# Every other quad of weight pieces of the gate and up products in Strassen's seven-product form

## The chip, the cores and the metric

The kernel runs on one core of one Trainium2 chip. The metric is the device time of one execution in microseconds (us). Three runs of the kernel before took 2240.97, 2241.1 and 2241.2 us, with 2241.1 us as the median. A core has TensorE (PE in the profile; PEld is its loading of stationary operands), VectorE (DVE), ScalarE (ACT), GpSimd (POOL) and SyncE (SP), which here issues the loads. Each engine works through its own instructions in a fixed order and waits where an operand or a buffer is not ready.

## The reference

One decoder layer over 256 tokens of width 2048 in float32. Two feed-forward blocks ("ffn1" and "ffn2", inner width 5632) stand before and after a mixing part (sliding-window attention beside a gated recurrence); a gated embedding and a last norm follow. Only the two feed-forward blocks are changed:

```python
def rmsnorm(x, w):
    return x * rsqrt(mean(x * x, axis=-1) + EPS) * w

def swiglu(h, w_gate, w_up, w_down):
    return (silu(h @ w_gate) * (h @ w_up)) @ w_down

x = x + 0.5 * swiglu(rmsnorm(x, ffn_norm), w_gate, w_up, w_down)
```

## The kernel before, in words

Every weight matrix comes from memory in pieces of 128 partitions x 1024 float32 values (512 KB): two blocks of 128 rows by 512 columns. Each value is used as a sum of two parts in a rounded float32 format. `Weights.prep` makes them for piece i: a DMA into `raw` (six buffers), a copy by ScalarE into `whi` (line 83, five buffers), and a subtraction on VectorE, `wlo` = `raw` - `whi` (line 84, five buffers). The activations are split the same way into a high and a low part (`hT*`, `act`).

The product of one piece with the activations takes twelve matmuls of 128 x 512 (`mm_a`): for each of the piece's two row blocks and each half `t` of the tokens, high by high (L241), low by high (L242), high by low (L247). The sums of a block of 512 output columns stand in two PSUM banks `pa`, one for each token half, out of four with the tag "acc"; four more with the tag "misc" serve transposes and small products.

The feed-forward block takes the inner width in 11 groups `c` of 512 columns. A group has eight gate and eight up pieces. ScalarE applies SiLU to the gate sums (L303), VectorE multiplies with the up sums (L310), and two later steps transpose the result on TensorE (L284) and split it into `act` (L285, L286). After six groups, and after the other five, the down products of those groups follow, and VectorE adds their sums to `x` (L317). The norm's scale 1/rms is applied after the gate and up products, so that they can begin on the unscaled input; for ffn1 that input also comes already transposed from memory (`xT`).

The weights stand in one list, `weight_order`, in which they are used. `Weights.next` hands out the next piece and first calls `prep` for up to four pieces ahead (AHEAD); the instructions of a prep get a high priority. Work such as the transposes is put off by a number of pieces with `W.later`. A scheduler then lists the instructions of each engine once, at build time, by these priorities and by its own estimate of when each could start; on the chip the order is fixed. The change touches `Weights.prep`, `FF_SLICES`, `weight_order`, `ffn`, `next_stage` and what comes before the two blocks.

## Time and profile before

| what | value |
|---|---|
| median of three runs | 2241.1 us |
| the profiled execution's own time | 2238.86 us |
| its span, first to last instruction | 2236.9 us |
| mean granted TensorE clock | 0.999 of full speed |
| PE busy | 2220.7 us (99%) |
| DVE busy | 1204.4 us (54%) |
| ACT busy | 1028.7 us (46%) |
| memory traffic | 187 GB/s on average |

One execution is profiled. "Busy" counts the time in which at least one instruction of the engine was under way; a matmul's record (some 390 ns) is longer than the distance between two of them, since they overlap in the array, so that the distance of their starts is what one costs. The idle time before an instruction, and who ended it, stands behind "|" in tables and in brackets in timelines. An order of instructions is given in other rows, without times.

### The profile page before, as it was taken

The numbers are of one execution on the slowest core, as the hardware profiler recorded it, in microseconds if no ns is written. First come the engines' busy times: TensorE is split into PE (matmuls) and PEld (weight loads), VectorE is DVE, ScalarE is ACT, GpSimd is POOL, SyncE is SP. The second block draws the span as 40 slices with busy tenths as digits, with TensorE's granted clock in tenths as the row PEclk, the third lists the DMA queues.
The fourth block names the chain that finished last, engine by engine and source line by source line (L and its number), as shares of the span: only waits on it lengthen the run. The fifth ranks groups of instructions, "written<-read, shape, count | busy, mean of one in ns | idle before, by whom it ended". The sixth has DMA issues, their size and how long they took to land.

```text
span 2236.9 us, 27361 instructions
## 1 busy us (share of the span) xinstructions
PE 2220.7 (99%) x10620; PEld 1837.4 (82%) x10620; DVE 1204.4 (54%) x1416; ACT 1028.7 (46%) x1294; POOL 12.0 (1%) x25
## 2 busy tenths in 40 slices
PE   9999999999999999999999999999999999999998
PEld 7888888888888888877888888888888888888887
DVE  6555544454455576776455555544554444445555
ACT  6544433444444445556444445444443344444454
POOL 0000000000000000000000000000000000000000
PEclk9999999999999999999999999999999999999999
DMA  8666666666665555545666655566666666666663
GB/s 314 203 195 192 189 191 193 195 191 188 188 188 187 182 169 151 160 133 160 193 189 190 193 186 186 187 190 192 190 187 191 196 190 188 190 192 204 187 191 109
DMA packets 118066, 418.92 MB, mean 187 GB/s; under 512 B 13745, under 2 KB 14129, under 8 KB 117937
## 3 DMA queue, kind: packets, MB, share of 16 engines
q1 hardware_dynamic: 117072, 415.83, 60.6%
q8 instruction: 83, 1.36, 0.3%
q10 hardware_dynamic: 864, 1.35, 0.2%
q14 instruction: 47, 0.38, 0.0%
HBM read 415.03 MB, written 2.10 MB: 186 GB/s over the span
## 4 chain that ended last, share of the span: by engine, by line
PE 99%; ACT 0%; issue 0%; DMA 0%; DVE 0%; SPq 0%; ACTq 0%; POOLq 0%; POOL 0%
PE pa L241 31%; PE pa L242 30%; PE pa L247 30%; PE pb L262 3%; PE pb L264 1%; PE tp L284 1%; PE lv L631 1%; PE tx L332 0%; PE sc L549 0%; DMA raw<-in_ffn_gate 0%; PE po L588 0%; PE pb L266 0%; PE pt L574 0%; ACT s L564 0%; ACT whi L83 0%
## 5 line engine op out<-in xcount | busy, mean ns | idle before, releaser
L84 DVE TENSOR_TENSOR wlo<-raw,whi 128x1024 fp32r<-128x1024 f32 (+1 forms) x781 | 955.2, 1223 | 928.5 <-ACT whi L83 924.4
L83 ACT CAST whi<-raw 128x1024 fp32r<-128x1024 f32 (+1 forms) x781 | 821.9, 1053 | 1114.2 <-PE pa L242 1039.1
L241 PE MATMUL pa<-whi,hTf 128*128 128x512 f32 x1408 | 552.8, 393 | 5.5 <-ACT whi L83 5.5
L242 PE MATMUL pa<-whi,hTf 128*128 128x512 f32 x1408 | 549.0, 390 | 0.0
L247 PE MATMUL pa<-wlo,hTf 128*128 128x512 f32 x1408 | 376.8, 389 | 0.0
L241 PEld LDWEIGHTS pa<-whi,hTf 128*128 128x128 f32 x1408 | 264.9, 188 | 60.2 <-ACT whi L83 6.2
L247 PEld LDWEIGHTS pa<-wlo,hTf 128*128 128x128 f32 x1408 | 264.4, 188 | 55.1
L242 PEld LDWEIGHTS pa<-whi,hTf 128*128 128x128 f32 x1408 | 265.0, 188 | 53.9
L241 PE MATMUL pa<-whi,act 128*128 128x512 f32 x704 | 275.9, 392 | 0.0
L242 PE MATMUL pa<-whi,act 128*128 128x512 f32 x704 | 274.1, 389 | 0.0
L241 PE MATMUL pa<-whi,hTmx 128*128 128x512 f32 x480 | 192.1, 400 | 0.0
L247 PE MATMUL pa<-wlo,act 128*128 128x512 f32 x704 | 188.3, 389 | 0.0
L242 PE MATMUL pa<-whi,hTmx 128*128 128x512 f32 x480 | 187.4, 391 | 0.0
L247 PEld LDWEIGHTS pa<-wlo,act 128*128 128x128 f32 x704 | 132.2, 188 | 27.5
L242 PEld LDWEIGHTS pa<-whi,act 128*128 128x128 f32 x704 | 132.2, 188 | 26.9
L241 PEld LDWEIGHTS pa<-whi,act 128*128 128x128 f32 x704 | 132.2, 188 | 26.9
L247 PE MATMUL pa<-wlo,hTmx 128*128 128x512 f32 x480 | 128.4, 389 | 0.0
L241 PEld LDWEIGHTS pa<-whi,hTmx 128*128 128x128 f32 x480 | 90.1, 188 | 21.4 <-issue 2.5
L247 PEld LDWEIGHTS pa<-wlo,hTmx 128*128 128x128 f32 x480 | 90.1, 188 | 18.9
L242 PEld LDWEIGHTS pa<-whi,hTmx 128*128 128x128 f32 x480 | 90.2, 188 | 17.4
L262 PE MATMUL pb<-hTmx,whi 128*128 128x512 f32 x240 | 67.6, 400 | 0.0
L241 PE MATMUL pa<-whi,hTpl 128*128 128x512 f32 (+1 forms) x160 | 53.9, 348 | 0.0
(207 smaller groups left out, 1471.7 us busy)
## 6 DMA issues: line engine op xcount, KB each, us to landing
raw<-in_ffn_up SPq DMA_DIRECT2D x176, 512.0 KB, 3.6
raw<-in_ffn_down SPq DMA_DIRECT2D x176, 512.0 KB, 3.6
raw<-in_ffn_gate SPq DMA_DIRECT2D x175, 512.0 KB, 3.6
raw<-in_w_ga SPq DMA_DIRECT2D x32, 512.0 KB, 3.5
raw<-in_w_gb SPq DMA_DIRECT2D x32, 512.0 KB, 3.5
raw<-in_w_out SPq DMA_DIRECT2D x32, 512.0 KB, 3.5
raw<-in_ple_gate SPq DMA_DIRECT2D x32, 512.0 KB, 3.7
raw<-in_w_i SPq DMA_DIRECT2D x16, 512.0 KB, 3.6
```

Of the source, the lines that this page charges most:

```text
L83: nc.scalar.copy(hi[:, c], raw[:, c])
L84: nc.vector.tensor_tensor(lo[:, c], raw[:, c], hi[:, c].bitcast(F32), op=ALU.subtract)
L241: nc.tensor.matmul(ps[t], ks[:, 0, tok], hi[:, c], start=(j == 0 and c == 0), stop=False)
L242: nc.tensor.matmul(ps[t], ks[:, 1, tok], hi[:, c], start=False, stop=False)
L247: nc.tensor.matmul(ps[t], ks[:, 0, tok], lo[:, c], start=False, stop=(last and c == 1))
L262: nc.tensor.matmul(ps, hi[:, c], mov(c), start=(first and c == 0), stop=False)
L264: nc.tensor.matmul(ps[:, 0:S], lo[:, c], mov(c)[:, 0], start=False, stop=False)
L284: nc.tensor.transpose(pt[:, c, t * P:(t + 1) * P], srcs[t][:, i * P:(i + 1) * P], ident)
L631: nc.tensor.matmul(ps[a * 64:a * 64 + 64, i], k[:, c], q[:, c], start=True, stop=True)
```

## The change

In 21 of the 22 groups (all but the first of ffn1) the gate and up products are made together. A "quad" is two gate pieces and two up pieces of the same four row blocks; a group has four. The quads alternate (PATTERN = "SPSP"): "P" quads are multiplied as before. "S" quads are read as a 2 x 2 matrix of blocks (row halves by gate and up), which is multiplied with the 2 x 2 matrix of activations (token halves by row halves) in the seven-product form of Strassen and Winograd. The seven weight operands are three of the four pieces and four sums of pieces (L101, VectorE, in place in `raw`); `prep` makes a high and a low part of each of the seven ("role" 0 to 6). One role takes six matmuls. The sums stand in eight banks over both kinds of quad: P1, P2, Q3, Q6 in "acc", Q7, Q5, P4 and PE_ in "misc"; P2, P4, Q3 and PE_ also take the P quads' sums. One ScalarE copy and eight VectorE operations (L402) make gate and up results out of them.

Since a product of this form mixes token halves, the activations have to be scaled by 1/rms before: `scaled_parts` scales `x`, transposes it on TensorE (L342), and for S quads forms four differences and splits them (L369, L373, L374). For ffn1 this is put off to pieces 9 to 12 of the first group, which still multiplies `hT` from `xT`, and the loads of `x` are moved forward; for ffn2 the scale comes from the first three quarters of `x`, and a factor for the rest is applied after the products. Loads are taken out of `prep` (`load`) and run three pieces ahead (LEAD) with eight `raw` buffers. The down products come in five slices per block, each of groups finished earlier. `hT` now lies in the pool of `act` tiles (23 instead of 17).

```diff
-ACTS = 17
+LEAD = 3
+ACTS = 23
...
+        if key[0] == "S":
+            _, first, second, q, role = key
+            if role > 3:
+                return
+            (name, nb), kg = ((first, 2 * q), (first, 2 * q + 1), (second, 2 * q + 1), (second, 2 * q))[role]
+            idx = (kg, nb)
...
+            raw = self.raws[i] = self.tile("raw", i, 8, F32)
+            n = 1024 // parts
+            for p in range(parts):
+                c = slice(p * n, (p + 1) * n)
+                self.nc.sync.dma_start(raw[:, c], src[:, c])
...
+        while self.loaded < min(i + 1 + (LEAD if i > 12 else 0), len(self.order)):
+            self.load(parts)
...
+            role = key[-1] if key[0] == "S" else 0
+            raws = [self.raws.get(i - role + k) for k in range(4)]
+            src = raws[(0, 1, 2, 0, 2, 3, 1)[role]]
+            if role == 3:
+                b11, b21, b22, b12 = raws
+                add(b22, b12, b22)
+                add(b12, b11, b12)
+                add(b11, b11, b22)
+            elif role == 6:
+                add(raws[1], raws[1], raws[0])
+            hi, lo = self.tile("whi", i, 5), self.tile("wlo", i, 5)
...
+                nc.scalar.copy(hi[:, c], src[:, c])
+                nc.vector.tensor_tensor(lo[:, c], src[:, c], hi[:, c].bitcast(F32), op=ALU.subtract)
...
-FF_SLICES = [(0, 6), (6, 11)]
+FF_SLICES = (((0, 3), (0, 2)), ((3, 5), (2, 4)), ((5, 7), (4, 6)), ((7, 9), (6, 8)), ((9, 11), (8, 11)))
+PATTERN = "SPSP"
...
+                for q, kind in enumerate(PATTERN):
+                    if kind == "S":
+                        order.extend(("S", (g, c), (u, c), q, role) for role in range(7))
+                    else:
+                        order.extend((v, (2 * q + k, c)) for k in range(2) for v in (g, u))
...
+        xs = [etile(name="xs") for _ in range(2)]
+        for t in range(2):
+            nc.scalar.activation(xs[t], x[t][q], AF.Copy, scale=s[:, t:t + 1])
...
+        full = [atile([P, 4, 2, P], F32, name="af") for _ in range(2)]
...
+                nc.scalar.activation(quarter[:, kp, c], pt[:, c].rearrange("p (t n) -> p t n", t=2), AF.Copy, scale=gain[:, f:f + 1])
+        a11, a21, a12, a22 = (quarter[:, k, :, t] for k in range(2) for t in range(2))
+        a5, a6, a7, a3 = (full[1][:, i] for i in range(4))
+        for o, u, v in ((a5, a21, a22), (a6, a11, a5), (a7, a21, a11), (a3, a12, a6)):
+            nc.vector.tensor_tensor(o, u, v, op=ALU.subtract)
+        parts = []
+        for i in range(2):
+            hi, lo = (atile([P, 4, 2, P], name="as") for _ in range(2))
+            nc.scalar.copy(hi, full[i])
+            nc.vector.tensor_tensor(lo, full[i], hi.bitcast(F32), op=ALU.subtract)
+            parts.append((hi, lo))
...
+        mix = lambda i: lambda c: (ch[:, i, c], cl[:, i, c])
+        A[q] = (raw(0, 0), raw(1, 0), mix(3), mix(1), mix(2), mix(0), raw(1, 1))
...
+        P1, P2, Q3, Q6, Q7, Q5, P4, PE_ = range(8)
...
+                for role in range(7):
+                    hi, lo = (v.rearrange("p (c n) -> p c n", c=2) for v in W.next(("S", first, second, q, role)))
+                    for c in range(2):
+                        sh, sl = A[q][role](c)
+                        mm(role, sh, hi[:, c])
+                        mm(role, sl, hi[:, c])
+                    for c in range(2):
+                        mm(role, A[q][role](c)[0], lo[:, c])
+                if q == PATTERN.rindex("S"):
+                    tmp = atile([P, 2, 512], F32, name="st")
+                    p1, v2 = tmp[:, 0], tmp[:, 1]
+                    nc.scalar.copy(p1, banks[P1])
+                    tt(v2, banks[Q6], p1, ALU.subtract)
+                    tt(g[:, 1], banks[Q7], v2, ALU.add)
+                    tt(u[:, 0], banks[Q5], v2, ALU.add)
+                    tt(u[:, 1], banks[Q5], g[:, 1], ALU.add)
...
+                    for (name, nb), (b0, b1) in ((first, (P2, P4)), (second, (Q3, PE_))):
+                        hi, lo = (v.rearrange("p (c n) -> p c n", c=2) for v in W.next((name, (2 * q + k, nb))))
+                        for c in range(2):
+                            for t, b in enumerate((b0, b1)):
+                                tok = slice(t * P, (t + 1) * P)
+                                mm(b, A[q][k][:, c, 0, tok], hi[:, c])
+                                mm(b, A[q][k][:, c, 1, tok], hi[:, c])
+                        for c in range(2):
+                            for t, b in enumerate((b0, b1)):
+                                mm(b, A[q][k][:, c, 0, t * P:(t + 1) * P], lo[:, c])
+        tt(g[:, 0], banks[P2], p1, ALU.add)
+        last_first(g, 0)
+        tt(g[:, 1], banks[P4], g[:, 1], ALU.subtract)
+        last_first(g, 1)
+        tt(u[:, 0], banks[Q3], u[:, 0], ALU.add)
+        tt(u[:, 1], banks[PE_], u[:, 1], ALU.add)
+        return g, u
...
+                e, u = strassen_group((gate, c), (up, c), A, silu)
                 for t in range(2):
-                    nc.vector.scalar_tensor_tensor(e[t], pu[t], r[:, t:t + 1], e[t], op0=ALU.mult, op1=ALU.mult)
+                    if n == 1:
+                        nc.vector.tensor_tensor(e[:, t], u[:, t], e[:, t], op=ALU.mult)
...
-            W.later(5 + 2 * nb + t, lambda t=t, nb=nb: load_x(t, nb))
+            W.later(4 + nb, lambda t=t, nb=nb: load_x(t, nb))
...
+    for q in range(4):
+        W.later(9 + q, lambda q=q: scaled_parts(A1, q, r_first(), gains["ffn1"]))
...
+        if nb == 2:
...
+            nc.vector.tensor_reduce(v3, ss2[:, :, 0:3], axis=AX.X, op=ALU.add)
+            nc.vector.tensor_scalar(v3, v3, 1.0 / 1536, EPS, op0=ALU.mult, op1=ALU.add)
+            nc.gpsimd.tensor_tensor(s3, v3, nhalf[:, 0:2], op=ALU.pow)
+            nc.vector.tensor_tensor(v3, v3, s3, op=ALU.mult)
...
+            for q in range(3):
+                W.later(1 + 2 * q, lambda q=q: scaled_parts(A2, q, s3, gains["ffn2"]))
...
+            W.later(2, lambda: scaled_parts(A2, 3, scale2[0], gains["ffn2"]))
```

The scheduler's order of TensorE, within the second group of a slice. Before, the twelve matmuls of one gate piece (`whi_801`, `wlo_802`) go to two banks:

```order
L241 MATMUL pa_822<-whi_801,hTf_82 128x512
L242 MATMUL pa_822<-whi_801,hTf_82 128x512
L241 MATMUL pa_823<-whi_801,hTf_82 128x512
L242 MATMUL pa_823<-whi_801,hTf_82 128x512
L241 MATMUL pa_822<-whi_801,hTf_82 128x512
L242 MATMUL pa_822<-whi_801,hTf_82 128x512
L241 MATMUL pa_823<-whi_801,hTf_82 128x512
L242 MATMUL pa_823<-whi_801,hTf_82 128x512
L247 MATMUL pa_822<-wlo_802,hTf_82 128x512
L247 MATMUL pa_823<-wlo_802,hTf_82 128x512
L247 MATMUL pa_822<-wlo_802,hTf_82 128x512
L247 MATMUL pa_823<-wlo_802,hTf_82 128x512
```

Now two roles of an S quad (`as` are the activations' parts, `ps_2041` and `ps_2042` are P1 and P2):

```order
L399 MATMUL ps_2041<-whi_2137,as_493 128x512
L399 MATMUL ps_2041<-whi_2137,as_494 128x512
L399 MATMUL ps_2041<-whi_2137,as_493 128x512
L399 MATMUL ps_2041<-whi_2137,as_494 128x512
L399 MATMUL ps_2041<-wlo_2138,as_493 128x512 x2
L399 MATMUL ps_2042<-whi_2153,as_493 128x512
L399 MATMUL ps_2042<-whi_2153,as_494 128x512
L399 MATMUL ps_2042<-whi_2153,as_493 128x512
L399 MATMUL ps_2042<-whi_2153,as_494 128x512
L399 MATMUL ps_2042<-wlo_2154,as_493 128x512 x2
```

A prepared operand of an S quad lasts for six matmuls to one bank, one of before for twelve to two banks.

VectorE's order around the end of a group and the start of the next. Before (`ff_982` and `ff_983` take the products of the gate and up results, `act` is their split):

```order
L84 TENSOR_TENSOR wlo_1116<-raw_1114,whi_1115 128x1024 [waits DMAHW6_49,PE_49,Activation_49]
L310 SCALAR_TENSOR_TENSOR ff_982<-pa_986,rstdf_498,ff_982 128x512 [waits PE_49]
L84 TENSOR_TENSOR wlo_1140<-raw_1138,whi_1139 128x1024 [waits DMAHW7_49,PE_49,Activation_49]
L310 SCALAR_TENSOR_TENSOR ff_983<-pa_987,rstdf_498,ff_983 128x512
L84 TENSOR_TENSOR wlo_1158<-raw_1156,whi_1157 128x1024 [waits DMAHW0_49,PE_49,Activation_49]
L84 TENSOR_TENSOR wlo_1176<-raw_1174,whi_1175 128x1024 [waits DMAHW1_49,PE_49,Activation_49]
L286 TENSOR_TENSOR act_820<-tp_866,act_820 128x2x256 [waits Activation_49]
```

Now (`wlo_1999` belongs to role 2 of the next group's first S quad, `wlo_2018` to role 3, `wlo_2053`, `wlo_2065` and `wlo_2078` to roles 4 to 6; `ps_1710`, `ps_1715`, `ps_1711` are P2, P4 and Q3 of the ending group):

```order
L118 TENSOR_TENSOR wlo_1999<-raw_1946,whi_1998 128x1024 [waits DMAHW4_49,PE_49,Activation_49]
L101 TENSOR_TENSOR raw_1946<-raw_1964,raw_1946 128x1024 [waits DMAHW5_49,DVE_49]
L402 TENSOR_TENSOR ff_1716<-ps_1710,st_1958 128x512 [waits PE_49]
L101 TENSOR_TENSOR raw_1964<-raw_1922,raw_1964 128x1024 [waits DVE_49]
L402 TENSOR_TENSOR ff_1716<-ps_1715,ff_1716 128x512 [waits PE_49]
L101 TENSOR_TENSOR raw_1922<-raw_1922,raw_1946 128x1024 [waits DVE_49]
L402 TENSOR_TENSOR ff_1717<-ps_1711,ff_1717 128x512 [waits PE_49]
L101 TENSOR_TENSOR raw_1934<-raw_1934,raw_1922 128x1024 [waits DVE_49]
L118 TENSOR_TENSOR wlo_2018<-raw_1922,whi_2017 128x1024 [waits Activation_49]
L118 TENSOR_TENSOR wlo_2053<-raw_1946,whi_2052 128x1024 [waits PE_49,Activation_49]
L118 TENSOR_TENSOR wlo_2065<-raw_1964,whi_2064 128x1024 [waits PE_49,Activation_49]
L118 TENSOR_TENSOR wlo_2078<-raw_1934,whi_2077 128x1024 [waits PE_49,Activation_49]
```

The next group's four sums stand alternately with three results of the ending group, each of which waits for TensorE.

ScalarE's order in the first group of ffn1, where the gate sums `pa` are copied out and the up pieces are cast. Before:

```order
L206 ACTIVATE junk_322,ssf_85<-x_78 128x512
L298 COPY ff_336<-pa_160 128x512
L298 COPY ff_337<-pa_161 128x512
L83 CAST whi_343<-raw_342 128x1024
L83 CAST whi_364<-raw_363 128x1024
L83 CAST whi_385<-raw_384 128x1024
L83 CAST whi_406<-raw_405 128x1024
```

Now (`junk` are square sums of `x`, `xs` its scaled quarter, `tx` that quarter transposed):

```order
L459 COPY ff_356<-pa_168 128x512
L117 CAST whi_292<-raw_290 128x1024
L255 ACTIVATE junk_297,ssf_89<-x_75 128x512
L255 ACTIVATE junk_300,ssf_89<-x_79 128x512
L459 COPY ff_356<-pa_169 128x512
L117 CAST whi_316<-raw_314 128x1024
L255 ACTIVATE junk_321,ssf_89<-x_76 128x512
L255 ACTIVATE junk_324,ssf_89<-x_80 128x512
L350 ACTIVATE xs_371<-x_73,rstdf_367 128x512
L117 CAST whi_340<-raw_338 128x1024
L350 ACTIVATE xs_372<-x_77,rstdf_367 128x512
L117 CAST whi_363<-raw_361 128x1024
```

The last four square sums, which stood behind the first group's up pieces, and the scaling and splitting of `x` now stand between the casts of these pieces.

## Rows read from the trace of the kernel before

**Rows 1.** The page: busy time of each engine, with its share of the span, and VectorE's busy share and the granted clock, in tenths, over 40 slices of the span.

```profile
PE 2220.7 (99%) x10620; PEld 1837.4 (82%) x10620; DVE 1204.4 (54%) x1416; ACT 1028.7 (46%) x1294; POOL 12.0 (1%) x25
...
DVE  6555544454455576776455555544554444445555
...
PEclk9999999999999999999999999999999999999999
```

**Rows 2.** The waits of TensorE over the whole span: engine, line, waited for; us in total, times, longest.

```profile
PE pa L241 <- ACT whi L83: 5.5, 2, 5.3
PE pt L574 <- DVE s L568: 1.5, 2, 0.7
```

**Rows 3.** TensorE's timeline in a gate group of ffn1: start, duration, line, tile.

```profile
201.95 0.39 PE L241 MATMUL pa<-whi,hTf 128*128 128x512 f32 x1
...
203.76 1.07 PE L247 MATMUL pa<-wlo,hTf 128*128 128x512 f32 x4
```

**Rows 4.** VectorE's timeline in the same group; in brackets its idle time and who ended it.

```profile
199.61 1.23 DVE L84 TENSOR_TENSOR wlo<-raw,whi 128x1024 fp32r<-128x1024 f32 x1 [1.50 <-ACT whi L83]
202.33 1.23 DVE L84 TENSOR_TENSOR wlo<-raw,whi 128x1024 fp32r<-128x1024 f32 x1 [1.50 <-ACT whi L83]
```

**Rows 5.** Who waits for whom, ScalarE.

```profile
ACT whi L83 <- PE pa L242: 1039.1, 656, 2.8
```

**Rows 6.** Groups of instructions with their shapes: busy us, mean ns of one | idle time before them.

```profile
L84 DVE TENSOR_TENSOR wlo<-raw,whi 128x1024 fp32r<-128x1024 f32 x779 | 953.8, 1225 | 927.9 <-ACT whi L83 923.8 <-PE hp L681 1.5 <-PE pa L247 0.7
L317 DVE SCALAR_TENSOR_TENSOR x<-pa,x 128x512 f32<-128x512 f32 x32 | 22.0, 688 | 17.4 <-PE pa L247 17.4
...
L83 ACT CAST whi<-raw 128x1024 fp32r<-128x1024 f32 x779 | 820.7, 1054 | 1113.0 <-PE pa L242 1039.1 <-issue 21.7 <-PE pb L266 21.5
L303 ACT ACTIVATE ff<-pa,rstdf 128x512 f32<-128x512 f32 x42 | 26.7, 680 | 0.0
L206 ACT ACTIVATE junk<-x 128x512 f32<-128x512 f32 x38 | 23.9, 630 | 7.4 <-DVE x L317 2.8 <-DMA x<-in_x 2.5 <-DVE x L731 1.4
L201 ACT ACTIVATE hTf<-tx,vecs 128x256 fp32r<-128x256 f32 x16 | 7.5, 471 | 7.7 <-DVE hTf L202 6.7 <-PE tx L332 1.0
```

**Rows 7.** VectorE where several instructions stand ready behind each other: three subtractions merged into one row; an operation of 128x512 that reads PSUM, and the start of the next; a subtraction and two operations, of which the last needs the one before it.

```profile
33.77 3.50 DVE L84 TENSOR_TENSOR wlo<-raw,whi 128x1024 fp32r<-128x1024 f32 x3 [1.30 <-ACT whi L83]
...
949.43 0.68 DVE L581 TENSOR_TENSOR prev<-pt,cpT 128x512 f32<-128x512 f32 x1
950.03 0.73 DVE L612 TENSOR_SCALAR zs<-zs,omlb,lb 128x256 f32<-128x256 f32 x2
...
926.28 1.22 DVE L84 TENSOR_TENSOR wlo<-raw,whi 128x1024 fp32r<-128x1024 f32 x1
927.41 0.42 DVE L270 TENSOR_TENSOR z<-pb,z 128x256 f32<-128x256 f32 x1
927.87 0.42 DVE L272 TENSOR_TENSOR z<-z,rBmx 128x256 f32<-128x256 f32 x1
```

**Rows 8.** Busy time in the stretch of one group of ffn1 (us, then PE, PEld, DVE, ACT, POOL with counts, the clock, DMA share, GB/s).

```profile
97.00:140.60 43.60, 43.60 (x198) 36.12 (x197) 21.26 (x20) 19.21 (x20) 0.00 (x0) 1.00 0.62 188
```

**Rows 9.** TensorE and VectorE around four transposes: the first matmul behind four transposes of `ff`, the next such place one piece later.

```profile
234.60 0.60 PE L284 MATMUL tp<-ident,ff 128*128 128x128 f32 x4
234.95 0.48 PE L241 MATMUL pa<-whi,hTf 128*128 128x512 f32 x1
...
237.79 0.60 PE L284 MATMUL tp<-ident,ff 128*128 128x128 f32 x4
238.14 0.48 PE L241 MATMUL pa<-whi,hTf 128*128 128x512 f32 x1
```

**Rows 10.** The first group of ffn1: the stretch from 10 to 50 us as in rows 8, and ScalarE's timeline.

```profile
10.00:50.00 40.00, 40.00 (x178) 33.11 (x177) 27.71 (x32) 26.51 (x39) 0.00 (x0) 1.00 0.94 340
...
31.73 1.05 ACT L298 COPY ff<-pa 128x512 f32<-128x512 f32 x2
32.68 3.05 ACT L83 CAST whi<-raw 128x1024 fp32r<-128x1024 f32 x3
36.88 1.05 ACT L83 CAST whi<-raw 128x1024 fp32r<-128x1024 f32 x1 [1.15 <-PE pa L242]
```

**Rows 11.** GpSimd's power operation that makes 1/rms.

```profile
L213 POOL TENSOR_TENSOR rstdf<-rstdf,nhalf 128x2 f32<-128x2 f32 x2 | 1.4, 702 | 410.1 <-DVE rstdf L212 410.1
```

**Rows 12.** VectorE and ScalarE after a block of `w_out`, ahead of ffn2.

```profile
1326.61 0.69 DVE L731 TENSOR_TENSOR x<-pa,x 128x512 f32<-128x512 f32 x1 [1.09 <-PE pa L247]
1327.22 1.22 DVE L84 TENSOR_TENSOR wlo<-raw,whi 128x1024 fp32r<-128x1024 f32 x1
1328.35 0.69 DVE L731 TENSOR_TENSOR x<-pa,x 128x512 f32<-128x512 f32 x1
...
1329.65 0.63 ACT L206 ACTIVATE junk<-x 128x512 f32<-128x512 f32 x1
1330.18 0.19 ACT L206 ACTIVATION_READ_ACCUMULATOR junk<-x 128x1 f32 x1
```

**Rows 13.** DMA issues of the page: KB each, median us from issue to landing.

```profile
raw<-in_ffn_gate SPq DMA_DIRECT2D x175, 512.0 KB, 3.6
```

**Rows 14.** TensorE in the mixing part, four matmuls in a row into one bank.

```profile
763.65 1.09 PE L262 MATMUL pb<-hTmx,whi 128*128 128x512 f32 x4
```

More of the change, by code (lines that the diff above doesn't have):

```diff
@@ L64, in drain, with tile, load @@
             self.pump()
+    def tile(self, tag, i, bufs, dt=F32R):
+        return self.pool.tile([P, 1024], dt, tag=tag, name=f"{tag}{i}", bufs=bufs)
+    def load(self, parts=1):
+        i = self.loaded
+        self.loaded += 1
+        key = self.order[i]
+        if key[0] == "S":
[5 more added lines that the diff above has]
+        else:
+            name, idx = key
+        src = self.aps[name]
+        for j in idx:
+            src = src[j]
+        with self.tc.high_priority(offset=PRIO if i > 12 else 0):
+            raw = self.raws[i] = self.tile("raw", i, 8, F32)
[3 more added lines that the diff above has]
+                self.nc.sync.dma_start(raw[:, c], src[:, c])
     def prep(self, parts=1):
@@ L81, in prep @@
                 c = slice(p * n, (p + 1) * n)
-                nc.sync.dma_start(raw[:, c], src[:, c])
-                nc.scalar.copy(hi[:, c], raw[:, c])
-                nc.vector.tensor_tensor(lo[:, c], raw[:, c], hi[:, c].bitcast(F32), op=ALU.subtract)
+                nc.scalar.copy(hi[:, c], src[:, c])
+                nc.vector.tensor_tensor(lo[:, c], src[:, c], hi[:, c].bitcast(F32), op=ALU.subtract)
+        if key[0] != "S":
+            del self.raws[i]
+        elif role == 6:
+            for k in range(4):
+                del self.raws[i - 6 + k]
         self.ready[i] = (hi, lo)
@@ L192, in new_hT @@
     def new_hT(stage):
-        return [sb.tile([P, 4, 2, S], F32R, tag=f"hT{g}", name=f"hT{stage}{g}") for g in range(4)]
+        return [atile(name=f"hT{stage}") for _ in range(8)]
     def split_scaled(dst, src, g, vector=False):
@@ L292, in ffn, with to_act @@
+    def ffn(n, A, hT, r_of, on_block):
+        stat = lambda k: hT[k // 2][:, k % 2]
+        acts, es = {}, {}
+        def to_act(c, kp):
+            acts[2 * c + kp] = at = atile()
+            transpose_split(at, [es[c][:, t] for t in range(2)], kp)
+        for (a, b), (da, db) in FF_SLICES:
             for c in range(a, b):
-                pg = block_a(f"ffn{n}_gate", c, stat)
-                e = [etile(name="ff") for _ in range(2)]
-                early = n == 1 and c == 0
-                if early:
+                gate, up = f"ffn{n}_gate", f"ffn{n}_up"
+                if n == 1 and c == 0:
+                    pg = block_a(gate, c, stat)
+                    e = es[c] = atile([P, 2, 512], F32, name="ff")
@@ L314, in ffn @@
+                es[c] = e
+            late = []
+            for c in range(da, b):
+                for kp in range(2):
+                    if 2 * c + kp in acts:
+                        continue
+                    late.append(lambda c=c, kp=kp: to_act(c, kp))
+            for i, fn in enumerate(late):
+                if i < 2:
+                    fn()
+                else:
+                    W.later(i - 1, fn)
             for nb in range(4):
-                ps = block_a(f"ffn{n}_down", nb, lambda k: acts[2 * a + k // 2][:, k % 2], 2 * (b - a), 2 * a)
+                ps = block_a(f"ffn{n}_down", nb, lambda k: acts[k // 2 + 2 * da][:, k % 2], 2 * (db - da), 2 * da)
@@ L355, in load_xt @@
             k = 2 * i + c
-            split_scaled(hT[k // 4][:, k % 4], xt[:, c], gains["ffn1"][:, k:k + 1], vector=(c == 1 and i < 3))
+            split_scaled(hT[k // 2][:, k % 2], xt[:, c], gains["ffn1"][:, k:k + 1], vector=(c == 1 and i < 3))
     def load_in_order(dst, src):
```

119 lines of the change are left out of this document (84 added, 35 removed).

## The prediction

> **What bounds the kernel now.** I read the page first: TensorE is busy for 99% of the span, VectorE for 54%, ScalarE for 46%, and the granted clock is full in all slices [rows 1]. TensorE's waits add up to 7 us [rows 2]. So every piece costs what its matmuls cost: in a gate group the first and the ninth matmul of a piece start 1.81 us apart, 0.226 us each [rows 3], and the subtractions, one per piece, come every 2.72 us [rows 4], 0.2267 us for each of twelve. Behind TensorE the others wait: VectorE idles 1.50 us before each subtraction [rows 4], and ScalarE waited 1039 us in 656 casts for a buffer that TensorE had to free [rows 5]. A matmul less is worth its 0.2267 us, as long as VectorE and ScalarE still keep ahead; that is the question here, since the change moves work to them.
>
> **What is removed.** An S quad takes 7 x 6 = 42 matmuls instead of 4 x 12 = 48, a group 180 instead of 192. In 21 groups that is 252 matmuls, 57.1 us at 0.2267; a group's TensorE time falls from 43.5 to 40.8 us. In the orders shown, one role's six matmuls go to one bank, where pairs of before alternate. The nearest rows for a long run into one bank are those of the mixing part, (1.09 - 0.39) / 3 = 0.233 us [rows 14]; for 84 role matmuls in 21 groups the difference would be 12 us. There the moving operand is another tile, too, and the pairs in rows 3 share a bank without a loss, so I take 0.2267 and keep 12 us for the range; a gain per matmul has no row that speaks for it.
>
> The Trainium skill ("TensorE: Matmul & The Clock Gate", Part 1) gives 215.7 ns from start to start for 512 columns at full clock; the trace has 5% more, and the measurement decides. By the page's figure the 252 matmuls would be worth 54.4 us, and the forecast would be 2.7 us higher.
>
> **What is added on TensorE.** ffn1's activations are now transposed, 32 transposes; ffn2's were before, too. Four of them lengthen a piece from 2.72 to 3.19 us [rows 9], so 32 cost 8 x 0.47 = 3.8 us.
>
> **What is added on VectorE.** A subtraction lasts 1.225 us, but when several stand ready, three take 3.50 us, so one costs (3.50 - 1.225) / 2 = 1.137 us from start to start; an operation of 512 columns costs 0.60 us (949.43 to 950.03); one that needs the result just made starts 0.04 us after its end (927.41 + 0.42 to 927.87) [rows 6, 7]. The sums of pieces have the size of a subtraction; each needs the one in front of it, hence 1.265 us. A group then takes 22 x 1.137 + 8 x 1.265 + 10 x 0.60, with some 0.5 us for dependences: 41.6 us, where before it took 21.3 of 43.6 [rows 8]. That is 0.8 us more than TensorE's 40.8. But the excess lasts two or three groups, and ahead of each slice of gate and up work lie 16 down pieces with 1.5 us of free VectorE time each [rows 4], in which it gets ahead by as much as five buffers hold.
>
> So the local windows decide. A cast for piece n begins when the high matmuls of piece n-5 are over; the tightest window is that of role 3 at the start of a slice's second group. Let 0 be the start of the slice's first group. Role 2 takes the buffer of the second piece of the last P quad; its high matmuls end at 34.5 us, the cast takes one us, the subtraction ends at 36.7. Then come four sums and, between them, three results of the old group, which wait for TensorE [the second VectorE order above]: 36.7 + 4 x 1.265 + 3 x 0.60 + 0.2 = 43.8; role 3's subtraction ends at 44.9. TensorE wants that part after five pieces of work at 40.8 + 3 x 1.36 + 0.9 = 45.8. It fits by 0.9 us. In the middle of a group, without results in between, it fits by 2.8. At the start of a slice TensorE's order has roles 4 to 6 and half a P quad's first pieces ahead of roles 2 and 3, whose banks `x` still occupies; VectorE reaches the two additions to `x` (0.69 us each [rows 6]) after the third P piece's subtraction, at 9.1 us, TensorE needs the first at 9.75: a stall of about 0.1. Ten slice starts and eleven group ends with such margins I put at 5 us in all; ends 0 and 27 (below).
>
> ScalarE has 22 casts at 1.05 us and some 3 us more per group [rows 6], 26 of 40.8: no bound. Raw pieces: the same 512 KB loads land in 3.6 us [rows 13]; an S quad's four `raw` buffers come free by 6 us and the next quad's are read from 10 us on, so that nothing waits for memory.
>
> **The first group of ffn1.** This stretch is dense already: in 40 us ScalarE works 26.5 us [rows 10]. Moved in or added are four square sums (0.63 and a read of 0.19 us), eight scalings (as L303, 0.68), eight scalings with the gain and eight splits of P quads' halves (as L201, 0.47, less when back to back) and four casts of 1.05: about 17 us [rows 6, 12]. Together 43 of the 40 us. And they stand in front of casts for which TensorE waits: the copy of the gate sums now precedes two square sums and a cast, and holds ScalarE from about 27.4 to 29.5 us (before, it came at 31.73 without a wait [rows 10]); the first scaling waits for two small VectorE operations and the power, 0.70 us [rows 11]. TensorE's transposes of `xs` stand between its matmuls. Going through the order with these durations I find waits at the first transposes (1.5 us), at those of the second quarter (1.4), and behind them a late start of the roles 4 and 5 and of role 2's bank, which the product `ff` frees (4 to 6). I take 10 us; ends 0 (the casts get ahead as before) and 20 (all of the 17 us on the path).
>
> **The start of ffn2.** Four transposes stand two pieces (5.4 us) behind the third block of `w_out`. In rows 12 the second addition to `x` ends 2.4 us after the block's end would release the first, the square sum and its read take 0.8, then follow the mean, the power (0.70 [rows 11]) and two scalings of 0.68: 6 to 7 us, a wait of 1 to 2 us. Then `x`'s last additions stand among four sums and six subtractions, and role 3 needs the bank of the second: about 8.4 us after the slice begins, where TensorE is there at 5.4. Together 6 us, ends 0 and 10.
>
> **The sum,** against the profiled execution's 2238.9 us: - 57.1 + 3.8 + 10 + 6 + 5 = 2206.6. The median of the runs lies 2.2 us above the profiled one, so 2209 us. Its own range, with the single bounds combined, is 2200 to 2220.
>
> **Rivals.**
> (1) The order has slack and nothing waits: TensorE idles for 7 us in the whole trace [rows 2] although ScalarE and VectorE are far from idle there. Against it: no slice of before has VectorE above 7 tenths [rows 1], and here it would be at 100%. 2241.1 - 57.1 + 3.8 = 2188 us.
> (2) VectorE sets the pace of gate and up groups: its 41.6 us plus 0.5 us at heads that wait for TensorE, with nothing left of the lead: 42.1 instead of 40.8, 27 us in place of the 5: 2231 us. For it: the sum itself; against it: the down pieces between.
> (3) VectorE's operations don't overlap: every one waits for an event of ScalarE, of TensorE or of itself, and costs its full 1.225 + 0.04 us. A group takes 30 x 1.265 + 10 x 0.73 = 45.3 us, more than the 43.5 of before; 21 x 1.8 = 38 us slower, with the 3.8, 10 and 6 of above 2299 us, and less by what is worked ahead in the down pieces. It decides from 42.6 us a group on, where the gain is spent. Against it speak the 3.50 us for three subtractions, each of which waits for a cast [rows 7]. The Trainium skill ("VectorE: DVE Perf Modes", The DRAIN you can't avoid) says that the next operation doesn't start until the pipeline is empty, which would be this case; the trace shows starts some 0.09 us before the end of the one in front, as the page's later section on instructions without a wait allows.
>
> **Chances.** Forecast 0.52, (1) 0.20, (2) 0.18, (3) 0.10. The range of 2188 to 2236 us holds the first three almost whole. A difference of 0.2%, 4.5 us, is about what a measurement of this kernel can tell. Faster by more: the first three less 0.04 that lies near 2241: 0.86; within: 0.04; slower: 0.10.
>
> **What would show it.** Right: in gate and up groups VectorE's busy share near 100% and groups of 41 us; TensorE's waits of some 20 us, most in the first 80 us and where ffn2 begins; 10400 matmuls or so, still at 0.227 us. Wrong: waits of TensorE for `wlo` of role 3 (its line for VectorE, L118) of over 1 us in each group would mean (2) or (3); VectorE's back-to-back subtractions 1.26 us apart would mean (3); matmuls at 0.233 us in S quads would mean the bound that I set aside.

## The result, and the profile after

The changed kernel takes 2217.7 us (median of four runs, 2216.8 to 2218.4) beside 2241.0 us before on the same chip; the ratio is 0.9897, with a 95% interval of 0.988 to 0.9914. The forecast was 2209 us, the gain 23.3 us in place of 32. The profiled execution took 2218.1 us, its span 2216.0 us.

The page of the profile after, with the lines that answer to [rows 1]:

```profile
PE 2182.4 (98%) x10400; PEld 1795.3 (81%) x10400; DVE 1666.3 (75%) x1954; ACT 1168.4 (53%) x1482; POOL 12.7 (1%) x26
...
DVE  6987979789796566776455555898897979789654
PEclk9999999999999999999999999999999999999999
```

TensorE has its fewer matmuls and is still nearly always busy; VectorE stands at 7 to 9 tenths wherever gate and up products are made, but not at its limit. The clock's line hides something, since each of its slices is 55 us long.

TensorE's six largest waits after (engine, line, waited for; us in total, times, longest), for [rows 2]; five smaller groups, 4.0 us together, follow:

```profile
PE pa L290 <- ACT whi L117: 6.1, 2, 5.4
PE pa L291 <- DVE act L335: 3.9, 2, 2.8
PE ps L399 <- ACT whi L117: 3.8, 4, 2.6
PE ps L399 <- DVE wlo L118: 2.5, 3, 1.3
PE ps L399 <- DVE ff L464: 2.1, 1, 2.1
PE pt L751 <- DVE s L745: 1.5, 2, 0.7
```

The first row (the first weights of the program) and the last were there before. The others are new, and each comes a few times only: none belongs to every group.

Stretches after (columns as in [rows 8]: PE, PEld, DVE, ACT, POOL with counts, then the clock): a steady slice with its two groups and 16 down pieces, two single groups, and the three stretches of low clock, which lie in or right behind waits.

```profile
204.00:329.90 125.90, 125.90 (x564) 103.81 (x563) 107.18 (x108) 66.31 (x70) 0.00 (x0) 1.00 0.57 201
...
329.90:370.70 40.80, 40.80 (x181) 33.45 (x180) 38.67 (x38) 23.38 (x24) 0.00 (x0) 1.00 0.57 206
370.70:411.50 40.80, 40.80 (x181) 33.70 (x180) 39.45 (x39) 24.96 (x27) 0.00 (x0) 1.00 0.66 241
...
155.40:162.20 6.80, 6.09 (x14) 4.81 (x15) 5.32 (x25) 2.71 (x5) 0.00 (x0) 0.50 0.12 42
...
1401.30:1408.10 6.80, 5.64 (x14) 4.45 (x15) 3.42 (x6) 3.01 (x5) 0.70 (x1) 0.50 0.74 284
114.50:117.90 3.40, 3.40 (x10) 2.64 (x9) 2.50 (x4) 1.81 (x3) 0.00 (x0) 0.50 0.75 301
```

In a steady slice TensorE is busy for 125.90 of 125.90 us: nothing waits. A group takes the forecast's 40.8 us, with VectorE at 38.7 to 39.5 us of it. The last three rows are what the forecast had not: the granted clock is 0.50 there, 1.2 instead of 2.4 GHz, for 17.1 us in all. Two of them hold 14 matmuls in 6.8 us, where 30 have room at 0.2267. Part of that is waiting. The low clock itself shows in 31 matmuls that start 0.43 us behind the one in front instead of 0.2267: 1.6, 2.6 and 2.0 us in the order of time, 6.2 us lost together.

VectorE's timeline after: a slice's start in steady state, the first group of ffn1's new form, the end of that group, and the end of ffn1's first slice.

```profile
326.10 5.01 DVE L101 TENSOR_TENSOR raw<-raw,raw 128x1024 f32<-128x1024 f32 x4
331.04 8.04 DVE L118 TENSOR_TENSOR wlo<-raw,whi 128x1024 fp32r<-128x1024 f32 x7
339.00 1.28 DVE L491 SCALAR_TENSOR_TENSOR x<-pa,x 128x512 f32<-128x512 f32 x2
...
59.10 6.89 DVE L118 TENSOR_TENSOR wlo<-raw,whi 128x1024 fp32r<-128x1024 f32 x6
...
66.91 0.75 DVE L464 SCALAR_TENSOR_TENSOR ff<-pa,rstdf,ff 128x512 f32<-128x512 f32 x1
...
105.89 6.89 DVE L118 TENSOR_TENSOR wlo<-raw,whi 128x1024 fp32r<-128x1024 f32 x6
112.70 0.68 DVE L402 TENSOR_TENSOR ff<-ps,st 128x512 f32<-128x512 f32 x1
...
151.54 1.28 DVE L473 TENSOR_TENSOR ff<-ff,ff 128x512 f32<-128x512 f32 x2
155.01 0.17 DVE L585 TENSOR_TENSOR lmx<-hlb 128x8 f32<-128x8 f32 x1 [2.19 <-DMA hlb<-in_hlb]
...
155.38 0.68 DVE L335 TENSOR_TENSOR act<-tp,act 128x512 fp32r<-128x512 f32 x1
```

And what TensorE does meanwhile:

```profile
64.91 0.73 PE L399 MATMUL ps<-wlo,ap 128*128 128x512 f32 x2 [0.60 <-DVE wlo L118]
67.72 0.50 PE L399 MATMUL ps<-whi,as 128*128 128x512 f32 x1 [2.07 <-DVE ff L464]
...
111.70 0.73 PE L399 MATMUL ps<-wlo,ap 128*128 128x512 f32 x2 [0.62 <-DVE wlo L118]
113.44 1.25 PE L399 MATMUL ps<-whi,as 128*128 128x512 f32 x4 [1.00 <-DVE ff L402]
...
156.11 1.22 PE L291 MATMUL pa<-whi,act 128*128 128x512 f32 x2 [2.85 <-DVE act L335]
...
1399.97 1.19 PE L399 MATMUL ps<-whi,ap 128*128 128x512 f32 x4 [2.62 <-ACT whi L117]
1402.46 1.22 PE L399 MATMUL ps<-wlo,ap 128*128 128x512 f32 x2 [1.30 <-DVE wlo L118]
```

The product L464, which frees role 2's bank, stands behind six subtractions and three differences; TensorE waits 2.07 us for it. At 155 us VectorE's next instruction prepares constants of the mixing part (`hlb`, 8 KB). Its load has not landed, and all that is queued behind it, the split of `act` first, waits for 2.19 us. The last two rows are ffn2's start, where TensorE waits for a cast of ScalarE and then for a subtraction.

The excess of the gaps between two matmuls' starts (those over 0.45 us, less 0.2267) comes to 2.9 us before and 23.9 after, 21.0 more. The forecast's 10 + 6 + 5 is the same, but its parts are not:

| place after (us) | excess | forecast |
|---|---|---|
| first group of ffn1 and roles 4, 5, 2 behind it (15 to 78) | 4.5 | 10 |
| rest of the first new group and its end (78 to 120) | 3.6 | in the 5 |
| end of ffn1's first slice, constants (150 to 163) | 4.4 | none |
| start of ffn2 (1365 to 1410) | 6.0 | 6 |
| end of ffn2's first group and slice (1410 to 1530) | 2.0 | in the 5 |
| all other slices | 0.0 | in the 5 |

With 0.5 us more at the program's start this is 21.0. Of the span: - 57.1 + 3.8 + 21.0 + 6.2 at half clock = - 26.1; the trace has - 20.9, so that 5.2 us are in no term. Gaps of 0.24 to 0.45 us, too short for the table, hold 2.7 of them; the rest stays open.

### The profile page after: what moved, and what is told of

Same layout as the page of the kernel before. It is cut to its first block, busy times and chain, and to the rows that moved or that the text cites. A ratio compares the mean times of both kernels' runs of the same rounds, so it can differ in the third digit from the quotient of the medians.

```text
span 2216.0 us, 27978 instructions
## 1 busy us (share of the span) xinstructions
PE 2182.4 (98%) x10400; PEld 1795.3 (81%) x10400; DVE 1666.3 (75%) x1954; ACT 1168.4 (53%) x1482; POOL 12.7 (1%) x26
## 4 chain that ended last, share of the span: by engine, by line
PE 94%; DVE 3%; DMA 1%; ACT 1%; issue 1%; POOL 0%; SPq 0%; ACTq 0%; POOLq 0%; DVEq 0%
PE ps L399 38%; PE pa L290 16%; PE pa L291 16%; PE pa L296 16%; PE pb L311 3%; PE pb L313 1%; DVE wlo L118 1%; PE tp L333 1%; PE lv L808 1%; DMA raw<-in_ffn_gate 1%; ACT whi L117 1%; DVE raw L101 1%; DMA x<-in_x 0%; PE tx L506 0%; PE sc L726 0%
## 5 line engine op out<-in xcount | busy, mean ns | idle before, releaser
L118 DVE TENSOR_TENSOR wlo<-raw,whi 128x1024 fp32r<-128x1024 f32 (+1 forms) x907 | 1079.4, 1219 | 446.1 <-ACT whi L117 440.9
L399 PE MATMUL ps<-whi,ap 128*128 128x512 f32 x1344 | 337.2, 389 | 3.2 <-ACT whi L117 3.2
L399 PE MATMUL ps<-whi,as 128*128 128x512 f32 x1176 | 318.8, 393 | 4.3 <-DVE ff L464 2.1
L399 PEld LDWEIGHTS ps<-whi,ap 128*128 128x128 f32 x1344 | 251.6, 188 | 57.5 <-ACT whi L117 4.5
L399 PEld LDWEIGHTS ps<-whi,as 128*128 128x128 f32 x1176 | 220.9, 189 | 55.8 <-ACT whi L117 3.0
L101 DVE TENSOR_TENSOR raw<-raw,raw 128x1024 f32<-128x1024 f32 x168 | 205.4, 1223 | 4.2
L399 PE MATMUL ps<-wlo,ap 128*128 128x512 f32 x672 | 183.5, 390 | 2.5 <-DVE wlo L118 2.5
L399 PE MATMUL ps<-wlo,as 128*128 128x512 f32 x588 | 182.9, 392 | 0.0
L399 PEld LDWEIGHTS ps<-wlo,ap 128*128 128x128 f32 x672 | 126.1, 188 | 29.9 <-DVE wlo L118 3.8
L399 PEld LDWEIGHTS ps<-wlo,as 128*128 128x128 f32 x588 | 110.5, 189 | 24.4 <-DVE wlo L118 1.7
```

Source lines behind the costliest of these rows:

```text
L101: add = lambda out, a, b: nc.vector.tensor_tensor(out, a, b, op=ALU.add)
L118: nc.vector.tensor_tensor(lo[:, c], src[:, c], hi[:, c].bitcast(F32), op=ALU.subtract)
L399: nc.tensor.matmul(bank(i), stat, mov, start=done[i] == 1, stop=done[i] == todo)
```

## The experiments

The stages of all runs, read from the starts of matmuls: ffn1 from the first matmul to the first on the mixing part's input, then the mixing part with ffn2 up to the last part, which takes 100.0 us throughout; and the time at half clock up to the last matmul, added up from stretches that last 3.41 or 6.83 us (one in e4 10.24). The last three columns are those of the one profiled execution.

| run | median us | ffn1 | mixing, ffn2 | at half clock |
|---|---|---|---|---|
| before | 2241.0 | 733.8 | 1388.2 | 0 |
| after | 2217.7 | 730.8 | 1370.2 | 17.1 |
| e1_constants | 2221.4 | 734.7 | 1370.2 | 20.5 |
| e2_ffn1_plain | 2222.7 | 736.7 | 1369.9 | 6.8 |
| e3_ffn2_plain | 2236.9 | 731.8 | 1388.5 | 6.8 |
| e4_gpsimd_sums | 2388.0 | 810.4 | 1460.9 | 105.8 |
| e5_constants_late | 2211.6 | 724.9 | 1369.3 | 10.2 |
| e6_starts | 2216.0 | 731.8 | 1366.9 | 10.2 |
| e7_fourth_sum_gpsimd | 2219.9 | 730.3 | 1371.2 | 6.8 |
| e8_one_more_sum | 2234.4 | 738.7 | 1378.5 | 13.7 |
| e9_ffn2_start | 2214.3 | 726.1 | 1369.4 | 6.8 |
| e10_two_plain_groups | 2205.4 | 718.8 | 1369.8 | 6.8 |
| e11_both_starts | 2206.6 | 719.0 | 1371.0 | 3.4 |
| e12_gpsimd_quarter | 2204.3 | 718.4 | 1368.6 | 3.4 |

**Each block alone.**

```diff
-                if n == 1 and c == 0:
+                if n == 1:            # e2; in e3: if n == 2 or c == 0
...
```

> ffn1's ten changed groups are multiplied in the plain form again (with the scale put in after the products, in the new slices), ffn2 keeps the new form. Theory A (a matmul is worth 0.2267 us, waits and half clock stand only at the two starts): + 120 x 0.2267 = + 27.2 for the matmuls, - 3.8 for 32 transposes, - 13 for ffn1's waits, - 5.1 for its half clock: 2217.7 + 5 = 2223 us. Rival B (the new slices, not the new form, bring ffn1's waits): they stay, 2217.7 + 27.2 - 3.8 = 2241 us.

> ffn2's eleven groups are multiplied in the plain form (with its norm's scale after the products, transposed as for the mixing part), ffn1 keeps the new form. Theory A: + 132 x 0.2267 = + 29.9, less ffn2's waits (7.9) and half clock (3.4): 2217.7 + 18.6 = 2236 us. Rival B (the half clock isn't bound to ffn2's waits and appears elsewhere): 2240 us. Together with the run before: what both blocks lose has to add up to the whole change, (2241.0 - t) of the two summed = 23 us within 4.

Measured 2222.7 and 2236.9 us, both as theory A has it. Beside the runs of before with them (2241.2 us), the new form gains 18.5 us in ffn2 alone and 4.4 in ffn1 alone, together 22.9 of the whole change's 23.3. What both runs share with the change, the new slices, the earlier loads and the buffers, would count twice in that sum; so it is worth nothing that these runs can tell. With ffn1 plain, in the same new slices, no half clock is left in ffn1: the waits come with the new form, not with the slices. A steady slice of two groups takes 87.9 us of gate and up work plain and 82.66 in the new form: 5.3 us for 24 matmuls, 5.44 by the forecast's price. So ffn1 gives most of its gain back within its first 160 us: 4.5 + 3.6 + 4.4 us in waits, 4.2 lost at half clock, 3.8 for transposes, of 27.2.

**The constants.**

```diff
-    W.later(60, mix_constants)
+    W.later(56, mix_loads)         # e5: 90
+    W.later(66, mix_constants)     # e5: 128
...
```

> The loads of the mixing part's constants stay near where they were (piece 56), what VectorE and ScalarE compute from them is put off to piece 66, in the middle of the first slice's down products. Theory A: the wait of VectorE for a small DMA at 155 us held up the split of `act`, cost TensorE its two gaps there (1.24 + 3.25 us) and, behind them, 6.8 us at half the granted clock (3.4 us); all of that goes: about 2217.7 - 7.9 = 2210 us, and no half clock near 155 us. Rival B: the transposes at the end of a first slice cost by themselves what ffn2's cost there (0.89 + 1.32 us), so that 2.3 us and the clock's 3.4 are gained: 2212 us. Rival C: the half clock has nothing to do with the wait and comes at the same place: 2213 us or more.

Measured 2221.4 us, slower than the change itself. The scheduler put the first of these instructions ahead of eight results on VectorE:

```profile
155.44 0.17 DVE L589 TENSOR_TENSOR lmx<-hlb 128x8 f32<-128x8 f32 x1 [3.85 <-DMA hlb<-in_hlb]
...
155.80 0.68 DVE L402 TENSOR_TENSOR st<-ps,st 128x512 f32<-128x512 f32 x1
```

```profile
157.74 2.31 PE L333 MATMUL tp<-ident,ff 128*128 128x128 f32 x8 [7.58 <-DVE ff L402]
```

A wait of 3.85 us for 8 KB became one of 7.58 us on TensorE. So the run tests none of its theories, as the wait stayed. A date in the program's order is no date in the engine's order.

> The loads of the mixing part's constants at piece 90 and the work on them at piece 128, far from the first slice's end, so that no small DMA can stand at the head of VectorE's order there. Theory A (the wait for `hlb` held up `act`, and the half clock followed the wait): the 1.24 + 3.25 us of gaps and the 3.4 us lost at half clock near 155 us go, 2210 us. Rival B (the transposes at a first slice's end cost 2.2 us by themselves, as in ffn2): 2212 us, no half clock there. Rival C (the half clock comes there whatever waits): 2213 us or more, with a half stretch near 155 us.

Measured 2211.6 us. The stretch at the end of ffn1's first slice, columns as above:

```profile
149.90:157.00 7.10, 5.96 (x27) 4.60 (x28) 5.73 (x9) 2.52 (x4) 0.00 (x0) 1.00 0.33 106
```

The half clock there went with the wait, so C falls; a gap of 1.42 us at the transposes remains, as B has it, so that of the 4.4 us there 3.2 belong to the constants. The constants cost the change 6.1 us.

**Order at the starts.**

```diff
+                    with tc.high_priority(offset=2 * PRIO):
                         for t in range(2):   # SiLU and product L464
...
-                W.later(1 + 2 * q, lambda q=q: scaled_parts(A2, q, ...
+                W.later((1, 4, 11)[q], lambda q=q: scaled_parts(A2, q, ...
```

with the fourth quarter at 9 instead of 2, and the last additions to `x` at the higher priority.

> Priorities and dates at the two starts alone: the product that frees role 2's bank in ffn1 (and the SiLU ahead of it) goes ahead of the subtractions, so do the last two additions to `x` ahead of ffn2; ffn2's third and fourth quarter of activations are made 6 and 7 pieces later, outside its first S quad's sums. Theory A (VectorE's order makes these waits): the 2.5 us at 65 us, the 3.0 and 1.7 us at 1397 to 1401 us and the 3.4 us of half clock behind them go: 2207 us. Rival B (VectorE has too much to do there in total, whatever comes first): the waits come back at the next role or group, 2213 to 2218 us.

Measured 2216.0 us (2212.9 to 2217.2), not distinguishable from the change: rival B. The wait for L464 is gone, but three others of up to 1.5 us for `ap` stand in its place, and ffn2's gap of 3.0 us came back as one of 2.3 us at its second S quad.

**How much VectorE has left.**

```diff
                 add(b11, b11, b22)
+                nc.vector.tensor_tensor(b11, b11, b11, op=ALU.max)
```

> One more VectorE operation of a sum's size (it leaves its operand as it is) in front of each role 3, 1.265 us more per S quad, 2.5 us per group: VectorE's work in a group rises to some 43.6 us, above TensorE's 40.8. Theory A (role 3's window decides; the forecast gave it 0.9 us at a slice's second group, 2.8 us in the middle of a group): about 0.4 us in each of ten slices and 1.3 us at each of the four dense places of the starts, 4 + 5 us and a half stretch or two: 2222 to 2230 us. Rival B (the sum of VectorE's work sets the pace, and the down pieces give back only what five buffers hold, 5 us a slice): 21 x 2.8 - 10 x 5 = 9 us or more, with waits in every second group, 2230 to 2275 us. Rival C (the margin is far wider than the forecast's 0.9 us): steady slices without a wait, 2218 to 2222 us.

Measured 2234.4 us. Steady gate and up work grew from 82.66 to 84.3 us per slice, at two places in each, role 3 of both S quads of the second group. One slice:

```profile
377.35 0.61 PE L400 MATMUL ps<-wlo,as 128*128 128x512 f32 x2
378.50 1.67 PE L400 MATMUL ps<-whi,as 128*128 128x512 f32 x6 [0.53 <-ACT whi L118]
...
398.64 0.61 PE L400 MATMUL ps<-wlo,as 128*128 128x512 f32 x2
399.66 1.68 PE L400 MATMUL ps<-whi,as 128*128 128x512 f32 x6 [0.41 <-ACT whi L118]
```

The first is the window that the forecast called the tightest, so A has the place, but not the size: 1.65 us a slice, not 0.4, since the second S quad, where it counted 2.8 us of room, now waits too. The time lies in B's range. VectorE got 4.5 to 5.0 us more to do per slice (four times 1.13 to 1.26) and TensorE lost 1.65: by this estimate about 3 us per slice was all the room that the change had left.

**Sums on GpSimd.**

```diff
-        add = lambda out, a, b: nc.vector.tensor_tensor(out, a, b, op=ALU.add)
+        add = lambda out, a, b: nc.gpsimd.tensor_tensor(out, a, b, op=ALU.add)   # e4: all; e7: role 6 alone
```

> The eight sums of pieces per group (L101) are made on GpSimd. Theory A (VectorE is dense only at the two starts, where sums stand between results): steady groups stay at TensorE's pace if one sum lasts below some 2.6 us on GpSimd (three of them fit into the 7.8 us that four sums and three results have on VectorE before role 3 is needed), and the waits at 105 to 112 us and at 1397 to 1401 us (4.2 and 5.7 us) and the half clock behind them (1.7 and 3.4 us) shrink: 2203 to 2217 us. Beyond 2.6 us each quad waits 3 x (T - 2.6): with T = 4 us, 42 x 4.2 = 176 us more. Rival B (VectorE sets the pace in steady groups as well): VectorE has 10 us less per group, so a gain in every one of the 21 groups, 2195 us or less.

Measured 2388.0 us. GpSimd's time for a sum, and what TensorE waited for:

```profile
L101 POOL TENSOR_TENSOR raw<-raw,raw 128x1024 f32<-128x1024 f32 x168 | 403.6, 2402 | 1017.8 <-DVE wlo L118 1007.9
```

```profile
PE ps L399 <- ACT whi L117: 59.1, 42, 7.0
PE ps L399 <- DVE wlo L118: 52.1, 42, 1.4
```

2.40 us is below the 2.6 of the expectation, and still each of the 42 S quads waits 2.65 us on average (111.2 / 42). On top 105.8 us pass at half clock, in which 185 matmuls start some 0.2 us late: 36 us lost. VectorE's 10 us less per group gained nothing, but with these new waits the run alone can't decide on rival B; against it stand the change's own steady slices, in which TensorE waits for nothing. Why the bound was wrong shows the next run.

> Only the fourth sum of each S quad, that of role 6, is made on GpSimd (2.40 us there); the three that role 3 waits for stay on VectorE. VectorE has 2.5 us less per group. Theory A (steady groups don't wait for VectorE, the windows around role 3 at the two starts do): no change in steady groups, up to 5 us at 105 to 112 us and at 1397 to 1401 us with the half clock behind: 2212 to 2217 us. Rival B (GpSimd slows VectorE, whose subtractions took 1.273 instead of 1.220 us beside it): 5 to 20 us slower, 2223 us or more. Rival C (steady groups are held by VectorE after all): 21 x 1 us or more gained, 2196 us.

Measured 2219.9 us, a steady slice's gate and up work 83.07 instead of 82.66 us. GpSimd and VectorE in one group:

```profile
370.49 2.41 POOL L112 TENSOR_TENSOR raw<-raw,raw 128x1024 f32<-128x1024 f32 x1 [19.77 <-DVE raw L101]
```

```profile
371.47 2.51 DVE L118 TENSOR_TENSOR wlo<-raw,whi 128x1024 fp32r<-128x1024 f32 x1
```

A subtraction beside the sum takes 2.51 instead of 1.22 us; it ends 1.08 us after the sum, as if it had begun then. TensorE loses 0.5 us behind it. That is rival B's mechanism, though the time lies between A's range and B's.

**The two starts, with the late constants.**

```diff
+                W.later((1, 4, 9)[q], ...            # e9: second and third quarter; the fourth at 7
...
-                if n == 1 and c == 0:
+                if n == 1 and c < 2:                 # e10
-        W.later(9 + q, lambda q=q: scaled_parts(A1, ...
+        W.later((12, 16, 20, 34)[q], lambda q=q: scaled_parts(A1, ...
```

> The late constants of e5, and at ffn2's start: the last two additions to `x` ahead of the subtractions, the third and fourth quarter of activations 4 and 5 pieces later, so that the third quarter's splits no longer stand among the four sums of the first S quad. Theory A (these splits, 1.14 us each, and the additions behind subtractions made the waits there): of 3.0 and 1.0 us of gaps and 3.4 us of half clock nearly all goes, 2211.6 - 7 = 2205 us. Rival B (as in e6: a later quarter makes a wait at the second S quad, 2 to 3 us with half clock behind it): 2208 to 2212 us.

Measured 2214.3 us, no gain over e5. The waits have moved, to the second S quad and to the second group:

```profile
1402.25 0.61 PE L399 MATMUL ps<-wlo,ap 128*128 128x512 f32 x2
1405.41 0.93 PE L399 MATMUL ps<-whi,as 128*128 128x512 f32 x3 [2.55 <-DVE ap L251]
```

```profile
1441.90 0.73 PE L399 MATMUL ps<-wlo,ap 128*128 128x512 f32 x2 [0.64 <-DVE wlo L118]
1443.64 0.73 PE L399 MATMUL ps<-whi,as 128*128 128x512 f32 x2 [1.00 <-DVE ff L402]
```

The second pair is, to 0.02 us, what TensorE waits in the change after ffn1's first new group (0.62 and 1.00 us). VectorE arrived behind there, and with 39 of 40.8 us to do in a group it has little room to catch up.

> The late constants of e5, and ffn1's second group is multiplied in the plain form as well, while the scaled activations are made over two groups (pieces 12, 16, 20 and 34) instead of four pieces. It costs 12 matmuls, 2.7 us. Theory A (ffn1's waits come from VectorE and ScalarE having the activations and the first S group to do at once): the gaps at 61 to 74 us (4.1 us) and at 104 to 113 us (3.3 us) and 1.7 us of half clock go: 2211.6 + 2.7 - 9.1 = 2205 us. Rival B (the first S group brings its waits wherever it stands, since VectorE's work in a group is as long as TensorE's): 2211.6 + 2.7 = 2214 us.

Measured 2205.4 us, theory A to 0.4 us. ffn1 is 6.1 us shorter than in e5 although it has 12 matmuls more. The run changes two things at once, the second group's form and the dates of the activations, so that the share of each stays open. Of the waits for `ps` these are left, at ffn2's start:

```profile
PE ps L399 <- ACT whi L117: 2.6, 1, 2.6
...
PE ps L399 <- DVE wlo L118: 0.4, 1, 0.4
```

> Both together: if the two places are independent and each theory A holds, 2211.6 - 7 + 2.7 - 9.1 = 2198 us; if only one of them holds, 2205 us; if neither, 2211 to 2214 us.

Measured 2206.6 us: only one of the two cures works, e10's.

```diff
+                W.later(1 + 2 * q, lambda q=q: scaled_parts(A2, q, s3, gains["ffn2"], nc.gpsimd if q == 2 else nc.vector))
...
```

> e10 (late constants, two plain groups in ffn1) and, at ffn2's start, work taken off VectorE instead of put off: the four differences and two splits of the third quarter of activations (4 x 0.40 + 2 x 1.137 = 3.9 us of VectorE) are made on GpSimd, and the last two additions to `x` stand ahead of the subtractions. Theory A (VectorE's amount of work at that start, 3 to 4 us too much, makes the waits, and putting it off only moves them, as e9 showed): the gaps of 3.0, 1.0 and 0.5 us and the 3.4 us of half clock go and nothing comes back in the second group: 2205.4 - 7 = 2198 us. Rival B (GpSimd, at some 2.4 us a split and 0.6 us a difference, is late for the second S quad): a wait of 2 to 3 us there, 2202 to 2206 us. Rival C (VectorE lacks more than these 3.9 us): the 4.2 us at the second group's start remain, 2203 us.

Measured 2204.3 us (2203.1 to 2205.7): no measurable gain over e10. GpSimd, VectorE and TensorE at ffn2's start:

```profile
1377.36 6.70 POOL L373 TENSOR_TENSOR as<-af,as 128x1024 fp32r<-128x1024 f32 x2
```

```profile
1376.84 9.56 DVE L101 TENSOR_TENSOR raw<-raw,raw 128x1024 f32<-128x1024 f32 x4
```

```profile
1387.14 1.30 PE L398 MATMUL ps<-whi,as 128*128 128x512 f32 x4 [3.94 <-DVE x L940]
```

Four sums took 9.56 instead of 5.01 us and held up the additions to `x` behind them. No rival had foreseen that; B's lateness of GpSimd didn't come. The 4.2 us at the second group didn't come back either, so that C falls: had the 3.9 us left VectorE without slowing it, theory A might have held, which stays open. e10 and e12 beat both kernels, at 0.984 of the time before (0.9824 to 0.9854 and 0.9826 to 0.9853).

## Why the prediction was right, and where its sum was not

**Right in direction and within its range, 8.7 us off in the time.**

- *What a matmul is worth.* Right: 40.8 us a group; per pair of groups the new form saves 5.3 us beside the plain one, 5.44 forecast. The bound of 0.233 us for runs into one bank was rightly set aside: 181 matmuls in 40.80 us.
- *VectorE's operations.* Right: four sums 5.01 us, hence (5.01 - 1.225) / 3 = 1.262 (1.265 forecast); seven subtractions 8.04 us, hence 1.136 (1.137). Rival (3) falls. The Trainium skill ("VectorE: DVE Perf Modes", The DRAIN you can't avoid) lets the next operation wait for an empty pipeline; the subtractions start some 0.09 us before the end of the one in front, and the rows decide.
- *The windows.* The order and place were right. The additions to `x` came 9.1 us after the slice's start, as reckoned, and TensorE didn't stall. e8 shows the forecast's tightest window to be one of the two that give way, and the one that loses more (gaps of 0.92 and 0.80 us between starts). Rival (2) falls for the change as it is (125.90 of 125.90 us busy), though some 3 us of work more per slice would have spent the room. Rival (1), in which nothing waits, falls by the 21.0 us of new gaps. Of the "5 us in all" for slice starts and group ends, steady slices took nothing; 3.6 us came in and behind ffn1's first new group and 2.0 in ffn2's first slice, nearly all at the transposes of its end. That VectorE had no lead there is how we read it.
- *The start of ffn2.* 6 us forecast, 6.0 found, but in good part by luck. The forecast had role 3 wait for the bank that the second addition to `x` frees; TensorE waited instead for a cast that stands behind the four sums (2.62 us) and for a subtraction (1.30), and its first transposes 0.6 us in place of 1 to 2. In e6 and e9 the work was put off and the additions went first, and the waits returned later, which points to the amount of VectorE's work there and not to the order of the additions; e12 leaves that open.
- *The first group of ffn1.* Mis-sized, 4.5 us instead of 10, at the places it named: 0.7 us at the first transposes (1.5 forecast), none at the second quarter's (1.4), 3.8 at the roles behind them and role 2's bank (4 to 6), and none of the rest.
- *The step that failed:* the sum took TensorE's clock as it was in [rows 1], full in every slice, and priced a wait at its own length. Here waits of 3 to 5 us came with 3.4 or 6.8 us at 1.2 GHz, 17.1 us in all, and these cost 6.2 us on top. That is about half of the 11.5 us between the profiled 2218.1 and the forecast's 2206.6; most of the rest are the 5.2 us that are in no term. That the waits themselves add up to the 21 us of the sum is luck: the first group's smaller term (5.5 us less) offsets the wait for the constants (3.2 us), which no step named, and smaller waits. Only half of the waits lie where the forecast put most of them, in the first 80 us and at ffn2's start (4.5 + 6.0 of 21.0). The 2.2 us that were added for the median were not there either: it lies 0.4 us below the profiled execution.

## What to carry to other kernels

Where one engine's work is made shorter by giving another just as much as fits, ask where that other engine builds its lead, and keep its dense one-time work (here scaled activations and constants) out of the first stretch that has none: late constants brought 6.1 us, and a second plain group with the activations spread over it, at a price of 2.7 us, as much again net. Work that was only put off by a few pieces came back as a wait later. Price a new wait of the matmul engine with the clock behind it, and look at that clock in narrow stretches, since the page's slices average it away.
